# Gated linear attention outputs turned by VectorE in 32x32 blocks instead of by TensorE

## The chip, the cores and the metric

The kernel runs on one core of one Trainium2 chip. The metric is device time in microseconds (us), as the median of several runs; a separate profiled execution gives the trace that is read here.

## What is computed

One step of a hybrid decoder layer, for a prompt of 1024 tokens and 8 sample tokens, with model width 1024. From the normalised input come, by one combined input projection, the inputs of three branches: gated linear attention (GLA), multi-scale pooling and cross-attention. Each branch is gated, projected, gated again and summed; then one output projection, a residual and a final norm. What the change touches is the end of the first branch:

```python
o, S = gla_chunked(q, k, v, log_a, S0)                # 4 heads, key width 128, value width 256
o = rmsnorm(o, gla_gain.reshape(GLA_HEADS, GLA_DV))   # per head, times a gain for each channel
br_gla = o * jax.nn.silu(gla_g)
...
bproj = jnp.einsum('btnw,nwd->btnd', branches, w_branch)
```

## The kernel before

The heavy products run in float32r, each as three matmuls of a high and a low part (`mm3`, lines 241 to 243). The input projection is done in 40 column pairs (`Pair`), each as seven products (`run_product`, j = 0 to 6) of sums and differences of weight blocks (names a11, a12, s1 to s4, a22, with h and l for the parts). Results stand with channels on partitions and time along the free dimension, in tiles named c; GpSimd (POOL) stores them to scratch in DRAM. Only about two tiles c are in use at a time. Each c is written in four pieces (L611 and L628, then L637 and L647) out of PSUM tiles named px, of which there are six.

Between the products of the projection stand small steps of the other branches, as filler on TensorE. `fill` takes steps from two streams by a count of slots and of costs that the generators `yield`, so the order of TensorE and of the loads on SyncE (SP) is written out by the program. The order on VectorE, ScalarE and POOL is made by a scheduler. The GLA runs in 16 chunks, four heads by four chunks of 256 tokens, in the middle of the program. For a chunk, `gla_gates` makes the decays, `gla_within` the masked scores (tile ak holds their high and low part and the transposed key), `gla_recur` the recurrence with the state st and the outputs. The outputs leave `gla_recur` as tile `on` with tokens on partitions (two blocks of 128 tokens by 256 channels), scaled by the norm on ScalarE (L973, two instructions for a chunk). `gla_out` turns them: four 128x128 TensorE transposes against an identity into a small PSUM tile (L987; the small PSUM tiles, pz, are two), two ScalarE copies to tile `go` with the head's gain as scale (L989), and one store of 256 KB to the scratch `mixsc` (L990), channels by time.

Later, for the eight gate pairs of each branch (`Pair` with `gated`), `mixed` loads the stored half rows, 128 channels by 512 tokens (L662, tile mix), and `finish` multiplies them by the SiLU of the gate (L574). The products go to `brsc`. In the last stage `branch_k` loads them again and `split` makes the high part on ScalarE (L222) and the low part on VectorE (L223) for the branch projection. The branches are projected in the order cross-attention, GLA, pooling.

The value projection already has a block transpose: pairs with `turned` transpose a 128x512 tile on VectorE in 32x32 blocks (L581, tile vt), and four stores of a quarter of it (L584) put the blocks in place.

Of the kernel before, what the change touches and what calls it, by code (L numbers as in the profile page):

```python
# [14 lines left out]
AF = mybir.ActivationFunctionType  # L15
ALU = mybir.AluOpType
AX = mybir.AxisListType

P = 128
D = 1024  # L20
T = 1024
# [3 lines left out]
NH = 4  # L25
DK = 128
DV = 256
# [6 lines left out]
CT = 256  # L34
# [13 lines left out]
def trunk_kernel(ctx: ExitStack, tc: tile.TileContext,  # L48
# [3 lines left out]
    nc = tc.nc  # L52
# [46 lines left out]
    def PZ():  # L99
        return ps.tile([P, 512], F32, tag="pz", name="pz", bufs=2)  # L100
# [13 lines left out]
    def R(shape, dt=F32, name="r"):  # L114

        return shaped(wk.tile([P, 512], dt, tag="ring", name=name, bufs=NR), shape)
# [20 lines left out]
    ident = cp.tile([P, P], F32, name="ident")  # L137
# [27 lines left out]
    ngain, ggain, pscale, bav = vec[:, 0:8], vec[:, 8:16], vec[:, 16:24], vec[:, 24:28]  # L165
# [35 lines left out]
    def scratch(n, name, shape):  # L201
        return [dr.tile(list(shape), F32, name=f"{name}{i}") for i in range(n)]
# [6 lines left out]
    q_scr, k_scr = (scratch(2, s, PAIR) for s in ("qsc", "ksc"))  # L209
    vt_scr = scratch(NH, "vtsc", (T, DV))  # L210
    u_scr, xq_raw = (scratch(4, s, PAIR) for s in ("usc", "xqsc"))
    mix_scr = [scratch(4, f"mixsc{n}_", (P, 2, T)) for n in range(3)]
    m_scr = [scratch(4, f"msc{n}_", PAIR) for n in range(3)]
    br_scr = [scratch(4, f"brsc{n}_", PAIR) for n in range(3)]

# [3 lines left out]
    def split(dst_hi, dst_lo, src, scale=None):  # L219

        if scale is None:
            last["hi"] = nc.scalar.activation(dst_hi, src, AF.Copy)  # L222
            last["lo"] = nc.vector.tensor_tensor(dst_lo, src, dst_hi.bitcast(F32), op=ALU.subtract)  # L223
        else:
            nc.scalar.activation(dst_hi, src, AF.Copy, scale=scale)
            nc.vector.scalar_tensor_tensor(dst_lo, src, scale, dst_hi.bitcast(F32), op0=ALU.mult, op1=ALU.subtract)
# [319 lines left out]
    def run_product(n):  # L546

        i, j = seq[n]
        p = pairs[i]

        def saved(acc, c, name):
            r = Q(name)
            nc.scalar.activation(r, acc[c][:, :QT], AF.Copy)  # L553
            return r

        def piece(t, h, c):
            return t[:, h, c * QT:(c + 1) * QT]

        def diagonal(x, e):

            if e == 0:
                return x[:, 0:16].rearrange("p (a b) -> p a b", b=4)[:, 0:4:3]
            return x[:, 4:12].rearrange("p (a b) -> p a b", b=4)

        def finish(t, e):
            rows = (slice(0, 4, 3), slice(1, 3))[e]
            if p.s0 is not None:
                nc.gpsimd.tensor_copy(diagonal(smp[:, NS * p.s0:], e), t[:, :, 512:HT])
            if p.gated:
                n, g = p.gated  # L570
                for i in range(2):
                    ch, hf = divmod((0, 3, 1, 2)[2 * e + i], 2)
                    m = p.mix[e][i]
                    nc.vector.tensor_tensor(t[:, i, :512], t[:, i, :512], m, op=ALU.mult)  # L574
                ss = diagonal(brs[n].rearrange("p k b -> p (k b)")[:, 2 * NS * g:], e)
                nc.vector.tensor_tensor(t[:, :, 512:HT], t[:, :, 512:HT], ss, op=ALU.mult)
            if p.turned:
                for i in range(2):
                    ch, hf = divmod((0, 3, 1, 2)[2 * e + i], 2)
                    r = R([512], name="vt")  # L580
                    nc.vector.transpose(r, t[:, i, :512])  # L581
                    for q in range(4):
                        c0 = ch * P + 32 * q
                        nc.gpsimd.dma_start(out=p.dst[512 * hf:512 * hf + 512, c0:c0 + 32].rearrange("(t r) c -> r t c", r=32),  # L584
                                            in_=r[32 * q:32 * q + 32].rearrange("r (t c) -> r t c", c=32))
                return
            nc.gpsimd.dma_start(out=p.dst[:, rows, :], in_=t)

        def gate(t, h):
            if p.gated:  # L590
                act(t[:, h], t[:, h], AF.Silu)

        def mixed(e):

            if p.gated:
                n, g = p.gated
                for i in range(2):
                    ch, hf = divmod((0, 3, 1, 2)[2 * e + i], 2)
                    p.mix[e].append(loaded(mix_scr[n][g][:, ch, 512 * hf:512 * hf + 512], [512], "mix"))

        if j == 0:
            p.x = [PX() for _ in range(2)]
            p.r1, p.mix = [], ([], [])
            for c in product(p.x, n, True):
                p.r1.append(saved(p.x, c, "r1"))
                yield
        elif j == 1:
            y = [PX() for _ in range(2)]
            p.e1 = E([2, HT], name="c1")
            for c in product(y, n, True):  # L610
                nc.vector.tensor_tensor(piece(p.e1, 0, c), y[c][:, :QT], p.r1[c], op=ALU.add)  # L611
                if c:
                    gate(p.e1, 0)
                yield
        elif j == 2:
            p.r2 = []
            for c in product(p.x, n, False):
                p.r2.append(saved(p.x, c, "r2"))
                yield
        elif j == 3:  # L620
            p.z = [PX() for _ in range(2)]
            mixed(0)
            for c in product(p.z, n, True):
                yield
        elif j == 4:
            for c in product(p.x, n, False):
                r3 = saved(p.x, c, "r3")
                nc.vector.tensor_tensor(piece(p.e1, 1, c), p.z[c][:, :QT], r3, op=ALU.add)  # L628
                if c:
                    gate(p.e1, 1)  # L630
                    finish(p.e1, 0)
                yield
        elif j == 5:
            p.e2 = E([2, HT], name="c2")
            mixed(1)
            for c in product(p.z, n, False):
                nc.vector.tensor_tensor(piece(p.e2, 0, c), p.z[c][:, :QT], p.r2[c], op=ALU.add)  # L637
                if c:
                    gate(p.e2, 0)
                yield  # L640
        else:
            for c in product(p.x, n, False):
                dst = piece(p.e2, 1, c)
                if p.gated:
                    act(dst, p.x[c][:, :QT], AF.Silu)
                else:
                    nc.scalar.activation(dst, p.x[c][:, :QT], AF.Copy)  # L647
                if c:
                    finish(p.e2, 1)
                yield  # L650
# [6 lines left out]
    def mix_chunk(n, h, c):  # L657
        return mix_scr[n][h][:, :, c * CT:(c + 1) * CT]

    def loaded(src, shape, name, alloc=None):  # L660
        t = (alloc or R)(shape, name=name)
        nc.sync.dma_start(out=t, in_=src)  # L662
        return t
# [316 lines left out]

    def gla_out(h, c):
        on, _ = gla["o", h, c]
        g = R([2, CT], name="go")
        t = PZ()
        for i in range(2):
            for j in range(2):
                nc.tensor.transpose(t[:, i * CT + j * P:i * CT + (j + 1) * P], on[:, j, i * P:(i + 1) * P], ident)  # L987
        for i in range(2):
            nc.scalar.activation(g[:, i], t[:, i * CT:(i + 1) * CT], AF.Copy, scale=ggain[:, 2 * h + i:2 * h + i + 1])  # L989
        nc.gpsimd.dma_start(out=mix_chunk(0, h, c), in_=g)  # L990

    def gla_rows(h):

# [309 lines left out]
    with tc.issue_after(last["hi"].ins), tc.issue_after(last["lo"].ins):  # L1303
        prepare(1)
        for j in (4, 6):
            r = squares(x_t[j:j + 2], 4 + j)
# [35 lines left out]
    def branch_k(n, k):  # L1342
        hi, lo = E([2, HT], F32R, name=f"bh{n}"), E([2, HT], F32R, name=f"bl{n}")
        for hf in range(2):
            row = br_scr[n][k // 2][:, 2 * (k % 2) + hf]
            raw = loaded(row[:, :512], [512], "brr")
            split(hi[:, hf, :512], lo[:, hf, :512], raw)
        nc.sync.dma_start(out=brs[n][:, k].rearrange("p (h b) -> p h b", h=2),
                          in_=br_scr[n][k // 2][:, 2 * (k % 2):2 * (k % 2) + 2, 512:HT])
        split(hi[:, :, 512:HT], lo[:, :, 512:HT], brs[n][:, k].rearrange("p (h b) -> p h b", h=2))  # L1350
        return hi.rearrange("p h t -> p (h t)"), lo.rearrange("p h t -> p (h t)")
# [59 lines left out]
    for u, (o, n, d) in enumerate(units):  # L1411
# [4 lines left out]
        w, sig, acc = inputs.pop(u)  # L1416
# [56 lines left out]
    for hf, order in enumerate(ORDERS):  # L1473
        for tb in order:
            m = P if tb < 8 else NS
# [12 lines left out]
            if hf == 0:  # L1488
                x = (E([D], name="y") if tb < 8 else RAW("ys").rearrange("p a b -> p (a b)"))[:m]
                nc.sync.dma_start(out=x, in_=x_p[tb * P:(tb + 1) * P] if tb < 8 else x_s)  # L1490
                rows_[tb], sums[tb] = x, wk.tile([P, 4], F32, tag="yq", name="yq", bufs=9)[:m]
            x, sq = rows_[tb], sums[tb]
# [5 lines left out]
            n, a = hf, 0  # L1498
            for b in ends:
                t = ts if tb == 8 else begun.pop(0) if begun else PX()  # L1500
# [13 lines left out]
                n, a = n + 1, b  # L1514
# [3 lines left out]
            if end:  # L1518
                r = rstd_of(sq[:, 2:3], 1.0 / D, more=so_far)
# [41 lines left out]
```

## Time and profile before

| | |
|---|---|
| median of three runs | 1450.72 us (1450.0 to 1452.0) |
| the profiled execution | 1452.08 us, span 1450.2 us |
| granted TensorE clock | 0.999 |
| TensorE busy | 1421.7 us, 98% of the span |
| VectorE / ScalarE / POOL busy | 906.0 / 689.2 / 194.9 us |
| first and last transpose of `gla_out` on TensorE | 418.8 and 750.9 us |
| DMA | 259.42 MB, 179 GB/s on the mean |

A row of the groups and of the sources gives line, engine, operation, tiles as out<-in, and the count; then durations in ns (min/median/max), or the busy time in us, the mean of one in ns, and the idle time of the engine ahead of them with what ended it. A row of the timeline gives start and duration in us, and in brackets the idle time ahead and its releaser. PE is TensorE's matmul, PEld its weight load, DVE VectorE, ACT ScalarE.

### The profile page before, as it was taken

What the parts mean: (1) busy time and instruction counts of PE and PEld (TensorE: products, weight loads), DVE (VectorE), ACT (ScalarE), POOL (GpSimd) and SP (SyncE); (2) the same over time, 40 slices, a digit from 0 to 9 for tenths busy, and PEclk for the clock granted to TensorE, in tenths of its full rate; (3) what the DMA queues carried; (4) which work ended last, traced back from release to release, by engine and by line L of the source; (5) the groups of instructions that cost most, each with busy time, mean ns of one, the idle gap of its engine ahead of it and who ended that gap; (6) DMA issues with size and microseconds to landing.
All of it is one profiled execution on the core that took longest, in us unless ns stands there. A gap on an engine that the chain in (4) does not pass through costs nothing.

```text
span 1450.2 us, 28260 instructions
## 1 busy us (share of the span) xinstructions
PE 1421.7 (98%) x10753; PEld 1360.2 (94%) x10753; DVE 906.0 (62%) x2107; ACT 689.2 (48%) x1607; POOL 194.9 (13%) x353
## 2 busy tenths in 40 slices
PE   7999999998999999999999999999999999999998
PEld 6899999998899999999999999999999999999876
DVE  6956656666686767766756678785672434544436
ACT  6744435443465666656654445454472333233312
POOL 3112101124341111111111111110010000000000
PEclk9999999999999999999999999999999999999999
DMA  9346665666655453553544455455594677632633
GB/s 335 122 159 207 200 212 184 218 190 164 160 157 183 130 182 126 177 175 125 180 142 152 157 187 182 138 192 168 194 303 147 226 255 236 241 116 71 220 125 117
DMA packets 182739, 259.42 MB, mean 179 GB/s; under 512 B 21436, under 2 KB 131796, under 8 KB 182596
## 3 DMA queue, kind: packets, MB, share of 16 engines
q1 hardware_dynamic: 159900, 183.87, 41.4%
q0 software_dynamic: 22560, 73.56, 14.1%
q8 instruction: 84, 1.38, 0.4%
q14 instruction: 51, 0.42, 0.1%
q10 hardware_dynamic: 144, 0.20, 0.0%
HBM read 180.47 MB, written 77.56 MB: 178 GB/s over the span
## 4 chain that ended last, share of the span: by engine, by line
PE 86%; DMA 5%; DVE 5%; issue 2%; ACT 1%; SPq 0%; DVEq 0%; POOL 0%; ACTq 0%
PE px L241 25%; PE px L242 24%; PE px L243 24%; DMA qb<-xqs 2%; PE pz L243 2%; PE pz L242 2%; PE pz L241 2%; DMA raw<-in_w_in_dram 2%; DVE kc L769 1%; PE pz L403 1%; PE pz L955 1%; PE pz L936 1%; PE pz L809 1%; PE pz L938 1%; DVE ws L304 0%
## 5 line engine op out<-in xcount | busy, mean ns | idle before, releaser
L243 PE MATMUL px<-bh,wbl 128*128 128x384 f32 (+1 forms) x576 | 184.1, 320 | 0.0
L242 PE MATMUL px<-bl,wbh 128*128 128x384 f32 (+1 forms) x576 | 184.1, 320 | 0.0
L241 PE MATMUL px<-bh,wbh 128*128 128x384 f32 (+1 forms) x576 | 183.7, 319 | 0.0
L553 ACT ACTIVATE r<-px 128x258 f32<-128x258 f32 x240 | 90.0, 376 | 45.6 <-PE px L243 45.0
L241 PEld LDWEIGHTS px<-bh,wbh 128*128 128x128 f32 x576 | 108.3, 188 | 0.0
L242 PEld LDWEIGHTS px<-bl,wbh 128*128 128x128 f32 x576 | 108.2, 188 | 0.0
L243 PEld LDWEIGHTS px<-bh,wbl 128*128 128x128 f32 x576 | 108.2, 188 | 0.0
L241 PE MATMUL px<-ot,s1h 128*128 128x258 f32 x320 | 93.9, 293 | 0.0
L241 PE MATMUL px<-ot,s3h 128*128 128x258 f32 x320 | 93.4, 292 | 0.0
L241 PE MATMUL px<-o,s4h 128*128 128x258 f32 x320 | 93.2, 291 | 0.2 <-DVE c L628 0.2
L241 PE MATMUL px<-o,a11h 128*128 128x258 f32 x320 | 92.9, 290 | 0.0
L241 PE MATMUL px<-o,a12h 128*128 128x258 f32 x320 | 92.9, 290 | 0.0
L241 PE MATMUL px<-ot,a22h 128*128 128x258 f32 x320 | 92.9, 290 | 0.0
L241 PE MATMUL px<-ot,s2h 128*128 128x258 f32 x320 | 92.3, 288 | 0.0
L242 PE MATMUL px<-o,a11h 128*128 128x258 f32 x320 | 91.0, 284 | 0.3 <-DVE o L223 0.3
L243 PE MATMUL px<-o,a11l 128*128 128x258 f32 x320 | 90.6, 283 | 0.0
L242 PE MATMUL px<-ot,a22h 128*128 128x258 f32 x320 | 90.5, 283 | 0.0
L242 PE MATMUL px<-ot,s2h 128*128 128x258 f32 x320 | 90.0, 281 | 0.5 <-DVE ot L223 0.5
L243 PE MATMUL px<-ot,s3l 128*128 128x258 f32 x320 | 90.5, 283 | 0.0
L243 PE MATMUL px<-o,a12l 128*128 128x258 f32 x320 | 90.4, 283 | 0.0
L242 PE MATMUL px<-o,a12h 128*128 128x258 f32 x320 | 90.4, 283 | 0.0
L243 PE MATMUL px<-ot,s1l 128*128 128x258 f32 x320 | 90.4, 282 | 0.0
(470 smaller groups left out, 4616.0 us busy)
## 6 DMA issues: line engine op xcount, KB each, us to landing
raw<-in_w_in_dram SPq DMA_DIRECT2D x80, 512.0 KB, 4.0
msc<-c POOLq DMA_DIRECT2D x24, 516.0 KB, 4.3
brsc<-c POOLq DMA_DIRECT2D x24, 516.0 KB, 4.0
sig<-msc SPq DMA_DIRECT2D x24, 516.0 KB, 6.6
mix<-mixsc SPq DMA_DIRECT2D x48, 256.0 KB, 4.5
brr<-brsc SPq DMA_DIRECT2D x48, 256.0 KB, 5.2
wbr<-in_w_branch_dram SPq DMA_DIRECT2D x24, 512.0 KB, 6.1
acc<-sig POOLq DMA_DIRECT2D x16, 516.0 KB, 5.3
```

Of the source, the lines that this page charges most:

```text
L241: nc.tensor.matmul(out, lhsT=lh, rhs=rh, start=start, stop=False, skip_group_check=more)
L242: nc.tensor.matmul(out, lhsT=lh, rhs=rl, start=False, stop=False, skip_group_check=more)
L243: nc.tensor.matmul(out, lhsT=ll, rhs=rh, start=False, stop=stop, skip_group_check=more)
L403: nc.tensor.matmul(t[:, :DV], lhsT=memT[k // 2][:, k % 2, a * P:(a + 1) * P], rhs=raw[k // 2][:, k % 2], start=k == 0, stop=k == NK - 1)
L553: nc.scalar.activation(r, acc[c][:, :QT], AF.Copy)
L769: nc.vector.tensor_tensor_reduce(kc[:, a, :], kc[:, a, :], qb[:, bb, :], scale=1.0, scalar=0.0, op0=ALU.mult, op1=ALU.add, accum_out=sc[:, ...
L809: nc.tensor.matmul(t[32 * j:32 * j + 32, :DV], lhsT=pm[:, a, 4 * i + j, :], rhs=vc[j][:, a, :], start=a == 0, stop=a == 1)
L936: nc.tensor.matmul(t[0:64, 0:P], lhsT=ki[:, 0:64], rhs=qi, start=True, stop=True)
L938: nc.tensor.transpose(t[:, P:2 * P], kt, ident)
L955: nc.tensor.matmul(to, lhsT=kiqi[:, 1, cs], rhs=st, start=False, stop=True)
```

## The change

`gla_out` no longer uses TensorE, PSUM and ScalarE. One VectorE instruction transposes the chunk's 128x512 tile in 32x32 blocks, so that partition 32q+r holds channel 32b+r of the tokens 32q to 32q+31 of both token blocks j, for all eight channel blocks b. Four stores of 64 KB, one for each q, place these blocks in a new scratch `onsc`, in runs of 64 numbers (256 bytes). In that scratch a channel's 512 tokens lie together, but in the order q, chunk, token block. `mixed` reads the 512 numbers as before; `finish` multiplies through a view that puts the order right, in pieces of 32. The gain, which the removed ScalarE copies carried, becomes the scale of the first branch's `split` in `branch_k`: ScalarE's copy gets a scale, and VectorE's subtraction becomes a scalar-tensor-tensor instruction.

```diff
-    mix_scr = [scratch(4, f"mixsc{n}_", (P, 2, T)) for n in range(3)]
+    mix_scr = [None if n == 0 else scratch(4, f"mixsc{n}_", (P, 2, T)) for n in range(3)]
+    on_scr = scratch(NH, "onsc", (DV // 32, 32, 2, 4, 2, 64))
...
                     m = p.mix[e][i]
-                    nc.vector.tensor_tensor(t[:, i, :512], t[:, i, :512], m, op=ALU.mult)
+                    if n == 0:
+                        x = m.rearrange("p (q w k) -> p w q k", q=4, w=4)
+                        y = t[:, i, :512].rearrange("p (w q k) -> p w q k", q=4, w=4)
+                        nc.vector.tensor_tensor(y, y, x, op=ALU.mult)
+                    else:
+                        nc.vector.tensor_tensor(t[:, i, :512], t[:, i, :512], m, op=ALU.mult)
...
-                    p.mix[e].append(loaded(mix_scr[n][g][:, ch, 512 * hf:512 * hf + 512], [512], "mix"))
+                    src = (mix_scr[n][g][:, ch, 512 * hf:512 * hf + 512] if n else
+                           on_scr[g][4 * ch:4 * ch + 4, :, hf].rearrange("b r q c x -> (b r) (q c x)"))
+                    p.mix[e].append(loaded(src, [512], "mix"))
...
     def gla_out(h, c):
         on, _ = gla["o", h, c]
-        g = R([2, CT], name="go")
-        t = PZ()
-        for i in range(2):
-            for j in range(2):
-                nc.tensor.transpose(t[:, i * CT + j * P:i * CT + (j + 1) * P], on[:, j, i * P:(i + 1) * P], ident)
-        for i in range(2):
-            nc.scalar.activation(g[:, i], t[:, i * CT:(i + 1) * CT], AF.Copy, scale=ggain[:, 2 * h + i:2 * h + i + 1])
-        nc.gpsimd.dma_start(out=mix_chunk(0, h, c), in_=g)
+        g = R([512], name="go")
+        nc.vector.transpose(g.rearrange("p (b j k) -> p j b k", j=2, k=32), on.rearrange("p j (b k) -> p j b k", k=32))
+        for q in range(4):
+            nc.gpsimd.dma_start(out=on_scr[h][:, :, c // 2, q, c % 2].rearrange("b r x -> r b x"),
+                                in_=g[32 * q:32 * q + 32].rearrange("r (b x) -> r b x", b=8))
...
-            split(hi[:, hf, :512], lo[:, hf, :512], raw)
+            split(hi[:, hf, :512], lo[:, hf, :512], raw, None if n else ggain[:, k:k + 1])
```

How it moves instructions is seen at three places. The lines of the changed program are numbered a few higher.

TensorE at the last chunk, before: L1043 are the matmuls of the GLA's sample tokens, the others products of the projection.

```order
L243 MATMUL px<-o_501,a12l 128x258
L1043 MATMUL pz<-s_10022,pm 32x256 x2
L1043 MATMUL pz<-s_10026,pm 32x256 x2
L987 MATMUL pz<-ident,on 128x128 x4
L241 MATMUL px<-ot_705,s2h 128x258
L242 MATMUL px<-ot_706,s2h 128x258
```

The same place in the changed program:

```order
L244 MATMUL px<-o_501,a12l 128x258
L1048 MATMUL pz<-s_9980,pm 32x256 x2
L1048 MATMUL pz<-s_9984,pm 32x256 x2
L242 MATMUL px<-ot_705,s2h 128x258
L243 MATMUL px<-ot_706,s2h 128x258
```

The four transposes are gone and nothing else of TensorE's order has moved, here and at the other fifteen places.

VectorE at the second chunk, before: st is the GLA state, c a projection result, s the sample states, a11l and s4l low parts of weight factors, ws a sum of weight blocks.

```order
L304 TENSOR_TENSOR ws<-raw 128x512
L960 SCALAR_TENSOR_TENSOR st<-st,decp,pz 128x256
L611 TENSOR_TENSOR c_5848<-px,r_5720 128x258
L223 TENSOR_TENSOR a11l<-raw,a11h 128x512
L1026 SCALAR_TENSOR_TENSOR s_5963<-vb,smp,s_5963 128x256 x2
L223 TENSOR_TENSOR s4l<-ws,s4h 128x512
```

The same place in the changed program:

```order
L305 TENSOR_TENSOR ws<-raw 128x512
L968 SCALAR_TENSOR_TENSOR st<-st,decp,pz 128x256
L992 STREAM_TRANSPOSE go<-on 128x2x8x32
L224 TENSOR_TENSOR a11l<-raw,a11h 128x512
L619 TENSOR_TENSOR c_5845<-px,r_5703 128x258
L619 TENSOR_TENSOR c_5845<-px,r_5717 128x258
L1031 SCALAR_TENSOR_TENSOR s_5957<-vb,smp,s_5957 128x256 x2
L224 TENSOR_TENSOR s4l<-ws,s4h 128x512
```

The block transpose stands behind the state update, and the two additions into c stand behind it and a11l. At most of the other chunks, too, the transpose follows the state update or the next instruction.

POOL at the fifth chunk, before: s are sample states on their way out, usc and msc the scratch of projection results.

```order
L1027 DMA out_dram<-s_6882 128x2x256
L1027 DMA out_dram<-s_6886 128x2x256
L990 DMA mixsc_1_175<-go 256x1x256
L568 COPY smp<-c_6866 128x8
L587 DMA usc_169<-c_6866 128x1032
L587 DMA msc_0_194<-c_6975 128x2x516
```

The same place in the changed program:

```order
L1032 DMA out_dram<-s_6870 128x2x256
L994 DMA onsc_183<-go 32x8x64 x4
L569 COPY smp<-c_6854 128x8
L593 DMA usc_169<-c_6854 128x1032
L1032 DMA out_dram<-s_6874 128x2x256
L593 DMA msc_0_194<-c_6960 128x2x516
```

Four stores stand in place of one, ahead of the store of the result c, and one store of a sample state has moved behind that.

## The prediction

> **What bounds the kernel now.** I read four views in this order: the page's engine shares, the windows by stage, the waits of TensorE, and the timeline where the transposes stand.
>
> ```profile
> PE 1421.7 (98%) x10753; PEld 1360.2 (94%) x10753; DVE 906.0 (62%) x2107; ACT 689.2 (48%) x1607; POOL 194.9 (13%) x353
> ```
> TensorE is busy for all but 28.5 us of the 1450.2 us span. In the windows the columns after the length are busy us (and instructions) of PE, PEld, DVE, ACT and POOL, then clock, DMA share and GB/s.
>
> ```profile
> 310.00:418.00 108.00, 100.07 (x833) 94.54 (x833) 73.71 (x194) 50.97 (x128) 46.84 (x77) 1.00 0.63 166
> 420.00:760.00 340.00, 338.30 (x2771) 322.48 (x2770) 233.72 (x622) 213.08 (x596) 46.23 (x76) 1.00 0.48 157
> 760.00:1035.00 275.00, 275.00 (x2305) 274.77 (x2304) 195.54 (x425) 128.55 (x273) 30.67 (x53) 1.00 0.52 168
> 1060.00:1400.00 340.00, 339.82 (x2099) 328.30 (x2098) 152.52 (x291) 116.33 (x197) 16.44 (x29) 1.00 0.60 196
> ```
> The GLA chunks run in 420 to 760. There PE idles 1.7 us, VectorE is used to 69%, POOL to 14%, and the clock is full. The two stages behind it have no PE idle to speak of (0.0 and 0.2 us), so time saved on PE before them reaches the end. The whole idle time of PE in the GLA stage is two waits:
>
> ```profile
> PE pz L987 <- ACT on L973: 1.2, 1, 1.2
> PE pz L936 <- DVE ak L223: 0.4, 1, 0.4
> ```
> The first is a wait of the very transposes that the change removes.
>
> **The PE transposes, removed: 64 of them.** The line's own row gives durations, the timeline gives what they cost in the stream:
>
> ```profile
> L987 PE MATMUL pz<-ident,on x64: 270/272/328, 418.8 to 750.9; 128*128 128x128 f32 x64
> ...
> 441.88 0.28 PE L243 MATMUL px<-ot,s2l 128*128 128x258 f32 x1
> 442.00 0.60 PE L987 MATMUL pz<-ident,on 128*128 128x128 f32 x4
> 442.35 0.36 PE L241 MATMUL px<-ot,s2h 128*128 128x258 f32 x1
> 442.55 0.28 PE L242 MATMUL px<-ot,s2h 128*128 128x258 f32 x1
> ```
> A product matmul is recorded as 0.28 us but one starts every 0.12 us: records overlap, and starts are what counts. From 441.88 to the second product matmul behind the transposes is 0.67 us; without them it would be two steps, 0.24. So four transposes cost 0.43 us, not 4 x 0.272 = 1.09. Fifteen chunks: 15 x 0.43 = 6.5 us.
>
> The TensorE page of the Trainium skill ("TensorE: Matmul & The Clock Gate", Part 4: PE-mode transpose) gives about 275 ns for such a transpose in a kernel and says that access latency makes up most of it. The recorded 272 ns agrees, but the overlap in the starts denies that it is the price; that way of charging is a rival below.
>
> The sixteenth chunk waits. Here it is beside an ordinary place with the same sample matmuls (L1043) ahead:
>
> ```profile
> 443.73 0.28 PE L243 MATMUL px<-ot,s2l 128*128 128x258 f32 x1
> 443.94 0.64 PE L1043 MATMUL pz<-s,pm 128*32 128x256 f32 x8
> ...
> 444.73 0.28 PE L242 MATMUL px<-ot,s1h 128*128 128x258 f32 x1
> ...
> 748.12 0.28 PE L243 MATMUL px<-o,a12l 128*128 128x258 f32 x1
> 748.33 0.64 PE L1043 MATMUL pz<-s,pm 128*32 128x256 f32 x8
> 750.20 0.95 PE L987 MATMUL pz<-ident,on 128*128 128x128 f32 x4 [1.23 <-ACT on L973]
> ...
> 751.10 0.28 PE L242 MATMUL px<-ot,s2h 128*128 128x258 f32 x1
> ```
> From product matmul to second product matmul it is 1.00 us at the ordinary place and 2.98 at the last chunk: 1.98 us go, transposes and wait together. What comes behind on PE (left factor s2) was made long before. Sum of this part: 6.5 + 2.0 = 8.5 us.
>
> **VectorE: 16 block transposes, added.** The same operation on the same 128x512 stands in the trace for the value rows, and so do stores of a quarter of a turned tile:
>
> ```profile
> L584 POOL DMA_DIRECT2D vtsc<-vt x64: 649/649/752, 310.5 to 418.4; - x64
> L581 DVE STREAM_TRANSPOSE vt<-c x16: 699/703/711, 309.5 to 413.4; 128x512 f32<-128x512 f32 x16
> ...
> DMA to landing us min/median/max: 2.3/3.1/6.8
> ...
> L990 POOL DMA_DIRECT2D mixsc<-go x16: 661/674/712, 421.8 to 752.7; - x16
> ```
> 16 x 0.70 = 11.2 us, lifting VectorE from 233.7 to about 245 of 340 us. The write order differs (blocks of two row groups interleaved), so 0.70 is the lower bound; twice that is my upper one, since no row shows this pattern. I take 0.70, because the rows of this size on VectorE all stand near it. Is it covered? In the second chunk the new order puts it behind the state update (st):
>
> ```profile
> 435.90 0.91 ACT L973 ACTIVATE on<-on,rr 128x256 f32<-128x256 f32 x2 [0.81 <-DVE rr L264]
> ...
> 440.24 0.47 DVE L960 SCALAR_TENSOR_TENSOR st<-st,decp,pz 128x256 f32<-128x256 f32 x1
> ...
> 442.07 0.69 DVE L223 TENSOR_TENSOR a11l<-raw,a11h 128x512 fp32r<-128x512 f32 x1 [0.88 <-ACT a11h L222]
> ```
> Its input was ready at 436.81, so VectorE won't stall on it, and 0.88 us of idle follow. What is queued behind and matters to PE is the split of the scores (ak), needed by the recurrence. The tightest of the later chunks:
>
> ```profile
> 458.47 0.42 DVE L223 TENSOR_TENSOR ak<-pz,ak 128x256 fp32r<-128x256 f32 x1 [0.45 <-ACT ak L222]
> ...
> 462.44 0.28 PE L241 MATMUL pz<-vsh,ak 128*128 128x256 f32 x1
> ```
> 3.55 us lie between its end and its use, five transposes' worth. One place has none: PE's 0.4 us wait at L936 is for this ak's read of the PSUM tile. With PE 0.43 us per chunk earlier and VectorE not, up to 0.4 us of the saving may end there. I charge 0.2.
>
> **Gone from ScalarE:** 32 PSUM copies with the head scale. They only relieve it (SP's queue keeps its order; eight of its pairs of loads read the new scratch). PSUM has one small tile fewer per chunk, so the others come free sooner.
>
> **POOL: 64 stores for 16.** 48 more at 0.65 us make 31 us, 46 to 77 of 340. Behind the four stand the stores of the projection results (c), and a result's tile can only be rewritten when its store has landed. The slowest such store and the next write of that kind of tile:
>
> ```profile
> L587 POOL DMA_DIRECT2D usc<-c x1: 725/725/725, 505.5 to 505.5; - x1
> ...
> DMA to landing us min/median/max: 6.7/6.7/6.7
> ...
> 517.42 0.75 DVE L611 TENSOR_TENSOR c<-px,r 128x258 f32<-128x258 f32 x2
> ```
> Landed at 512.2, rewritten at 517.4: 5.2 us of slack against 4 x 0.65 - 0.67 = 1.9 us of delay. Cost nothing; if POOL were slower, c would be late next. The bytes are the same 4 MB, in 256-byte runs for 1 KB; the value rows' stores with half that run landed in 3.1 us, and the readers of these tiles start after 820 us:
>
> ```profile
> L662 SPq DMA_DIRECT2D mix<-mixsc x48: 319/382/1510, 820.2 to 1067.1; - x48
> ...
> L574 DVE TENSOR_TENSOR c<-c,mix 128x512 f32<-128x512 f32 x48 | 32.8, 686 | 7.0 <-ACT c L75 6.6 <-ACT r L553 0.4
> ...
> L1529 DVE SCALAR_TENSOR_TENSOR y<-y,rr,fg 128x512 f32<-128x512 f32 x14 | 9.9, 749 | 0.2
> ```
> **Gate product and split.** 16 of the 48 products (L574) now read both operands in pieces of 32. Between nothing and a doubling that is 0 to 16 x 0.69 = 11 us of VectorE in a stage where it idles 79; I take nothing. 16 splits of the first branch become a scalar-tensor-tensor, 749 for 686 ns: 1.0 us, in a stage with VectorE idle for 187 of 340 us; ScalarE's half takes a scale. Both off the path.
>
> **The sum:** 8.5 - 0.2 = 8.3 us. The profiled execution took 1452.08 us, 1.9 around its span; it would take 1443.8. It stands 1.4 above the median of the three runs, 1450.72; from that median the forecast is 1442.4. Bounds of the saving: 10 (PE's 0.4 us wait also goes, and the ends of the runs differ by a microsecond) down to 4 (first rival).
>
> **Rivals.**
> *The saving is part handed to new waits.* VectorE is 0.70 us later per chunk wherever no idle follows, as here, where the new order puts the transpose between the last two rows:
>
> ```profile
> 511.53 0.47 DVE L960 SCALAR_TENSOR_TENSOR st<-st,decp,pz 128x256 f32<-128x256 f32 x1
> 511.92 0.68 DVE L304 TENSOR_TENSOR ws<-raw 128x512 f32<-128x512 f32 x1
> 512.52 0.48 DVE L1026 SCALAR_TENSOR_TENSOR s<-vb,smp,s 128x256 f32<-128x256 f32 x1
> ```
> If half the chunks gave back their 0.43 us, 3.4 us: 1445.8. For it: VectorE's chain ends PE's wait at L936. Against: only one such wait in 340 us. If all gave it back, nothing measurable would be left beyond the last chunk's 2 us: 1448.9.
>
> *Transposes charged by duration:* 64 x 0.272 = 17.4 us, and the last chunk's wait of 1.98 - 0.43 = 1.5: 1431.8. The starts speak against it.
>
> *Slower: the POOL queue.* If the stores hold POOL, c lands late, VectorE can't empty the PSUM tiles, PE stops. From the emptying to the next use of those tiles there is further cover:
>
> ```profile
> 470.26 0.42 DVE L611 TENSOR_TENSOR c<-px,r 128x258 f32<-128x258 f32 x1
> ...
> 476.61 0.28 PE L241 MATMUL px<-o,a11h 128*128 128x258 f32 x1
> ```
> 5.9 us, with the 5.2 above 11.1. To end 0.2% (2.9 us) slower, 16 chunks must wait 11.2 us, 0.7 each: four stores of (0.67 + 11.1 + 0.7) / 4 = 3.1 us decide it, against 0.65 measured while VectorE was 68% busy (first window); at 3.3 us, PE loses 1.4 x 16 = 23 us: 1465. The SBUF page of the Trainium skill ("SBUF — State Buffer", SBUF: two separate sides) has a rule against this change: GpSimd cannot write descriptors while VectorE holds their shared port, and a store of 620 ns took 3100. By that the sum would come out near 1452; the rows L584 show no such store.
>
> **How the numbers follow.** A measurement of this kernel tells 0.2% (2.9 us) from no change, so faster means under 1447.8. Likeliest, 1441 to 1444: 0.66. Part given back, 1444 to 1447.8: 0.21. All given back: 0.06. By duration: 0.01. POOL slower: 0.04, and 0.02 for a small slowing that I can't name, of which half stays within. So faster 0.88, same 0.07, slower 0.05. The range 1440.7 to 1446.8 leaves out those last cases and the end of the second.
>
> **What would show it.** Line L987 gone and product matmuls in steps of 0.12 us there; PE busy in the GLA stage 7 us lower; the wait for on (L973) gone from PE's waits; 16 transposes near 0.70 us on VectorE, none waiting for on; 64 stores near 0.65 us. PE waiting for ak, s or a factor's low part, or VectorE waiting for a store of c, would prove the sum wrong, as would a PE idle of over 2 us in that stage.

## The result, and the profile after

The changed kernel takes 1444.15 us (median of 4 runs, 1442.07 to 1445.01), the kernel before 1451.36 us beside it (4 runs): a ratio of 0.9949, 95% interval 0.9932 to 0.9966. The prediction was 1442.4 us, 1440.7 to 1446.8.

The page's engine shares after, busy us and share of the span:

```profile
PE 1417.4 (98%) x10689; PEld 1356.1 (94%) x10689; DVE 916.2 (63%) x2123; ACT 679.0 (47%) x1575; POOL 222.1 (15%) x401
```

TensorE has lost 64 matmuls (10753 before), VectorE has 10.2 us more work, ScalarE 10.2 less, POOL 27.2 more. The windows of the same four stretches, with the prediction's columns:

```profile
310.00:418.00 108.00, 102.37 (x851) 97.47 (x850) 74.36 (x195) 51.28 (x129) 44.92 (x74) 0.98 0.63 168
420.00:760.00 340.00, 340.00 (x2785) 324.49 (x2784) 250.03 (x659) 206.23 (x575) 74.28 (x127) 1.00 0.53 164
760.00:1035.00 275.00, 275.00 (x2304) 274.77 (x2304) 195.83 (x420) 128.84 (x272) 30.65 (x53) 1.00 0.51 165
1060.00:1400.00 340.00, 339.82 (x2068) 326.79 (x2067) 149.18 (x285) 113.00 (x189) 15.64 (x28) 1.00 0.59 192
```

In the GLA stage TensorE is busy for 340.00 of 340 us (338.30 before): both of its waits are gone, the one of the removed transposes for `on` and the 0.4 us for `ak` at the scores. VectorE and POOL have taken the work over without TensorE waiting for either. Of the signs that the prediction named, PE's busy time in the stage fell by 7.6 us (from 337.3 to 329.7, between the matmuls of the table below); the page's total fell by only 4.3, since matmuls at a lower clock count as busy for longer (13 fill two microseconds where 19 did, in the windows of the last section). The first row's clock, 0.98 where it was 1.00, is taken up further down.

What the new instructions cost, from the rows of the sources (min/median/max ns; L992 is the block transpose, L994 its stores, L578 the gate product in pieces of 32, L580 the plain ones):

```profile
L992 DVE STREAM_TRANSPOSE go<-on x16: 702/705/715, 421.2 to 745.0; 128x512 f32<-128x512 f32 x16
L994 POOL DMA_DIRECT2D onsc<-go x64: 582/585/629, 423.9 to 747.7; - x64
L578 DVE TENSOR_TENSOR c<-c,mix x16: 683/686/694, 913.4 to 994.0; 128x512 f32<-128x512 f32 x16
L580 DVE TENSOR_TENSOR c<-c,mix x32: 684/691/697, 820.9 to 1072.4; 128x512 f32<-128x512 f32 x32
```

And TensorE's timeline where the last chunk stood. Before, the place between product a12 and product s2 took 2.98 us:

```profile
742.72 0.28 PE L244 MATMUL px<-o,a12l 128*128 128x258 f32 x1
742.93 0.64 PE L1048 MATMUL pz<-s,pm 128*32 128x256 f32 x8
743.50 0.39 PE L242 MATMUL px<-ot,s2h 128*128 128x258 f32 x1
743.72 0.28 PE L243 MATMUL px<-ot,s2h 128*128 128x258 f32 x1
```

From the product matmul at 742.72 to the second one behind, at 743.72, it is 1.00 us, the length of the ordinary place in the prediction.

Matmul starts mark the stages more sharply than fixed windows. I took the start of the same three matmuls in each trace: the product with s2 ahead of the GLA (414.8 us before), the product with s1 behind its last chunk (753.8), the first matmul of the branch projection (1078.0). The table, worked out from those starts and the spans, serves for the experiments too:

| kernel | ahead of the GLA | GLA | pooling | rest |
|---|---|---|---|---|
| before | 414.8 | 339.1 | 324.2 | 372.3 |
| changed | 416.7 | 329.7 | 324.2 | 372.6 |
| changed, run again | 416.3 | 329.7 | 324.2 | 372.3 |
| transposes of `on` put back | 413.6 | 339.7 | 323.9 | 372.2 |
| transposes of the identity added | 413.7 | 337.5 | 324.0 | 372.3 |
| ScalarE's copies put back | 416.2 | 331.6 | 325.6 | 372.3 |
| stores issued twice | 416.2 | 331.3 | 330.0 | 372.3 |
| twice, but not at the end | 411.6 | 330.6 | 324.2 | 373.2 |
| the keys turned too | 420.6 | 336.4 | 324.2 | 372.3 |
| cross-attention's end spread out | 411.1 | 330.3 | 332.9 | 372.2 |
| the same, plan raised to 499 | 409.8 | 331.6 | 324.2 | 372.2 |

The GLA stage became 9.3 us shorter and the two behind it kept their lengths. The profiled execution lost 1.9 us ahead of the stage, where the change has no instruction.

### The profile page after: what moved, and what is told of

Read it like the earlier page. It is cut to its first block, busy times and chain, and to the rows that moved or that the text cites. A ratio compares the mean times of both kernels' runs of the same rounds, so it can differ in the third digit from the quotient of the medians.

```text
span 1443.3 us, 28179 instructions
## 1 busy us (share of the span) xinstructions
PE 1417.4 (98%) x10689; PEld 1356.1 (94%) x10689; DVE 916.2 (63%) x2123; ACT 679.0 (47%) x1575; POOL 222.1 (15%) x401
## 4 chain that ended last, share of the span: by engine, by line
PE 88%; DMA 5%; DVE 5%; issue 1%; ACT 1%; SPq 0%; POOL 0%; DVEq 0%; ACTq 0%; POOLq 0%
PE px L242 25%; PE px L243 25%; PE px L244 25%; DMA qb<-xqs 3%; PE pz L244 2%; PE pz L243 2%; PE pz L242 2%; DMA raw<-in_w_in_dram 1%; DVE kc L777 1%; PE pz L963 1%; PE pz L404 1%; PE pz L944 1%; PE pz L817 1%; PE pz L946 1%; PE pz L907 0%
## 5 line engine op out<-in xcount | busy, mean ns | idle before, releaser
L242 PE MATMUL px<-ot,s1h 128*128 128x258 f32 x320 | 94.1, 294 | 0.0
L243 PE MATMUL px<-ot,s1h 128*128 128x258 f32 x320 | 90.8, 284 | 0.0
```

Of the source, the lines that this page charges most:

```text
L242: nc.tensor.matmul(out, lhsT=lh, rhs=rh, start=start, stop=False, skip_group_check=more)
L243: nc.tensor.matmul(out, lhsT=lh, rhs=rl, start=False, stop=False, skip_group_check=more)
```

## The experiments

Each ran against the kernel before on the same chip, on three chips in all; the median of the kernel before lies between 1451.1 and 1452.8 us there. So ratios compare better than times across experiments; "over the changed kernel" means over its rerun, 1441.75 us.

**The changed kernel, run again.** Nothing is edited; it is the base for the others.

> The changed kernel again, timed beside the experiments. Path theory (the gain is the TensorE steps of the 64 transposes and the last chunk's wait, everything added is hidden): 8.3 us below before, some 0.3 of them uncertain. Eaten-gain theory (VectorE or POOL give back a part): 7 us or less below.

Measured: 1441.75 us (1441.27 to 1444.18) against 1451.44, ratio 0.993 (0.9916 to 0.9944). The gain is 9.7 us here and 7.2 in the first comparison; the prediction's 8.3 lies between. The intervals overlap.

**TensorE's transposes put back beside the new way.**

```diff
         g = R([512], name="go")
+        t = PZ()
+        for i in range(2):
+            for j in range(2):
+                nc.tensor.transpose(t[:, i * CT + j * P:i * CT + (j + 1) * P], on[:, j, i * P:(i + 1) * P], ident)
```

Their result is not used.

> The changed kernel with the 64 TensorE transposes of the outputs put back, into a small PSUM tile that nothing reads; ScalarE's copies stay away, the block transposes and stores stay. Path theory: all of it comes back, 15 x 0.43 + 2.0 = 8.5 us above the changed kernel, at before's time. Relief theory (the gain came from ScalarE's 32 copies and from the small PSUM tiles that come free sooner): it stays within 1.5 us of the changed kernel.

Measured: 1449.85 us, ratio 0.9992 (0.998 to 1.0003), 8.1 over the changed kernel. All the rest of the change is in it, so nearly the whole gain is TensorE's. ScalarE's copies stay away here, and the GLA stage still takes 339.7 us, as long as before (339.1): in that stage the relief of ScalarE gained nothing that can be seen.

**The same transposes, of the identity instead of `on`**, so that they wait for no data:

```diff
+                nc.tensor.transpose(t[:, i * CT + j * P:i * CT + (j + 1) * P], ident, ident)
```

> As the run with the transposes put back, but they turn the identity, so that they wait for no output. Path theory: 16 x 0.43 = 6.9 us above the changed kernel, and 1.5 us below the run that turns the outputs, because the last chunk's wait does not come back. Charging by recorded duration: 64 x 0.272 = 17.4 us above. Relief theory: within 1.5 us of the changed kernel.

Measured: 1449.53 us, ratio 0.9984 (0.9975 to 0.9992), 7.8 over the changed kernel; its GLA stage is 7.8 longer too. The 1.5 us that were expected between this kernel and the last one are 2.1 us in their profiled GLA stages (337.5 and 339.7) but 0.3 in the medians, so the runs don't confirm them. TensorE's waits in 415 to 780 us, of the kernel with transposes of `on` and then of this one (line waited at, releaser, us in total, times, longest):

```profile
PE pz L944 <- DVE ak L224: 1.8, 2, 1.3
PE pz L996 <- ACT on L981: 0.4, 1, 0.4
```

```profile
PE pz L944 <- DVE ak L224: 0.4, 1, 0.4
```

Without the 0.4 us wait, 64 transposes cost 7.4 us, 0.46 for each four. The price read from starts was 0.43; the price by duration would have been 17.4 us in all. That rival has fallen.

**A second block transpose for each chunk**, its result unused:

```diff
+        nc.vector.transpose(R([512], name="g2").rearrange("p (b j k) -> p j b k", j=2, k=32),
+                            on.rearrange("p j (b k) -> p j b k", k=32))
```

> The changed kernel with a second block transpose of each chunk's outputs on VectorE, into a tile that nothing reads: 16 x 0.70 = 11.3 us more of VectorE in the GLA stage, some 265 of 335 us. Path theory: hidden, within 0.7 us of the changed kernel. Eaten-gain theory (VectorE's added work delays TensorE): at least 0.3 us per transpose shows, 5 us or more.

Measured: 1442.02 us, ratio 0.994 (0.9927 to 0.9953). Another 11 us on VectorE cost nothing measurable; the new work on VectorE is covered with as much again to spare.

**ScalarE's 32 scaled copies put back:**

```diff
+        g2 = R([2, CT], name="g2")
+        for i in range(2):
+            nc.scalar.activation(g2[:, i], on[:, i], AF.Copy, scale=ggain[:, 2 * h + i:2 * h + i + 1])
```

> The changed kernel with ScalarE's work put back: two scaled 128x256 copies for each chunk, from the outputs into a tile that nothing reads, 32 x 0.5 = 16 us of ScalarE; TensorE and PSUM untouched. Path theory: within 0.7 us of the changed kernel. Relief theory: most of the 7 us come back.

Measured: 1443.06 us, ratio 0.9941 (0.9927 to 0.9955), 1.3 over the changed kernel. The intervals overlap, so the runs don't settle it, but in its one trace the GLA and pooling stages are 3.3 us longer together, and it has waits that the changed kernel lacks:

```profile
PE pz L1066 <- ACT os L1060: 1.3, 1, 1.3
PE px L242 <- DVE c L636: 0.8, 2, 0.5
PE pz L944 <- DVE ak L224: 0.4, 1, 0.4
```

**The kernel before with only the gain moved** into the first branch's split:

```diff
-            nc.scalar.activation(g[:, i], t[:, i * CT:(i + 1) * CT], AF.Copy, scale=ggain[:, 2 * h + i:2 * h + i + 1])
+            nc.scalar.activation(g[:, i], t[:, i * CT:(i + 1) * CT], AF.Copy)
...
-            split(hi[:, hf, :512], lo[:, hf, :512], raw)
+            split(hi[:, hf, :512], lo[:, hf, :512], raw, None if n else ggain[:, k:k + 1])
```

> The kernel before with one part of the change: the head's gain moved from ScalarE's copies of the outputs into the first branch's split, everything else as before. Path theory: within 0.5 us of before. Rival: the 16 scalar-tensor-tensor splits show, 16 x 0.06 = 1 us above.

Measured: 1450.84 us, ratio 0.9996 (0.9987 to 1.0005): nothing, as the prediction had it.

**Each store four times**, the last three to scratch that nothing reads:

```diff
+            for scr in no_scr:
+                nc.gpsimd.dma_start(out=scr[h][:, :, c // 2, q, c % 2].rearrange("b r x -> r b x"),
+                                    in_=g[32 * q:32 * q + 32].rearrange("r (b x) -> r b x", b=8))
```

> The changed kernel with every store of a turned quarter issued four times, three of them to scratch that nobody reads: 16 stores or 9.4 us of POOL for each chunk, 192 x 0.585 = 112 us more, and 12 MB more of DMA. Path theory with the cover that the prediction worked out (5.2 us until a result tile is rewritten and 5.9 us until its PSUM tiles are needed): within 1 us of the changed kernel. POOL rival, if the cover is only the first 5.2 us: some 3.5 us of TensorE wait at most chunks, 20 us or more.

Measured: 1517.21 us, ratio 1.0461 (1.044 to 1.0481), 75 us over the changed kernel. Four stores at 0.58 are 2.3 us in place of one, under the 3.1 us that the prediction had called decisive, and the loss was far beyond its 23 us. TensorE waits for 53 us in 415 to 830 us, and the granted clock is 0.96 from 415 to 820 us, some 16 us more (0.04 x 405). The stores did not get slower, by their source row:

```profile
L995 POOL DMA_DIRECT2D onsc<-go x64: 582/582/637, 420.9 to 818.0; - x64
```

TensorE waits for the results c (its waits in 415 to 780 us):

```profile
PE px L243 <- DVE c L620: 32.0, 7, 8.4
PE px L243 <- ACT c L656: 12.9, 4, 4.3
```

One such wait in the timelines of POOL, VectorE and TensorE, in this order:

```profile
473.25 0.56 POOL L594 DMA_DIRECT2D usc<-c  x1
...
489.61 0.72 POOL L594 DMA_DIRECT2D usc<-c  x1
```

```profile
479.47 0.69 DVE L225 TENSOR_TENSOR s4l<-ws,s4h 128x512 fp32r<-128x512 f32 x1 [2.17 <-ACT s4h L224]
...
487.56 0.42 DVE L225 TENSOR_TENSOR ak<-pz,ak 128x256 fp32r<-128x256 f32 x1
487.90 0.75 DVE L620 TENSOR_TENSOR c<-px,r 128x258 f32<-128x258 f32 x2
```

```profile
488.37 0.39 PE L243 MATMUL px<-o,a11h 128*128 128x258 f32 x1 [2.67 <-DVE c L620]
```

TensorE waits for the addition into c. That addition waits for no store: no idle time stands ahead of it, and the last store of a c tile before it, issued at 473.25 us, landed at 477.5 us, 10 us earlier. VectorE even idled 2.17 us before 479.47. The addition just stands late in VectorE's order, behind the scores' split. In the traces 111 of VectorE's 2123 instructions stand elsewhere in its order than in the changed kernel. Nor does a store hold up the rest of the stage: of all the idle time of VectorE and ScalarE in 415 to 830 us, a landing store ended 0.8 us. So what TensorE waits for isn't a full POOL queue but results that stand late in the order that the scheduler made of the same work with twelve more stores per chunk in it. Only one of these waits was followed through, and that the scheduler counts the stores' time on POOL when it makes the order is argued, not shown.

**Each store twice.** The edit is the one above with one scratch. In the traces 30 of VectorE's instructions stand elsewhere than in the changed kernel. (The 113 and 733 of the expectation count lines of another listing, for this kernel and the one above.)

> The changed kernel, with each of the 64 stores of block-transposed outputs issued twice (the second into a scratch tensor that nothing reads), so that POOL issues 64 more stores of about 0.58 us, 37 us more in all. With four times the stores the time rose by 75 us, and the trace put that on VectorE's rows, which stood in another order; here VectorE's order differs from the changed kernel's in 113 rows only, against 733 there. Theory of the order: POOL itself has room, so the time stays within about 2 us of the changed kernel's 1442 to 1444. Rival, POOL's own load: the cost grows with the stores, a third of 75 us, so some 25 us more, about 1467.

Measured: 1451.45 us, ratio 0.9998 (0.9988 to 1.0008). Both theories missed: the whole gain is gone, but not 25 us. By the table 1.6 us are lost in the GLA stage and 5.8 behind it. TensorE's waits in 415 to 780 us show the second part:

```profile
PE pz L243 <- ACT dfh L224: 3.3, 1, 3.3
PE pz L945 <- DVE ak L225: 1.2, 2, 0.7
PE pz L244 <- DVE dfl L225: 0.3, 1, 0.3
```

dfh and dfl are the parts of the first pooling windows. Behind the first of these waits the clock is at half for 3.4 us (windows view, clock in the column behind POOL's), which costs (1 - 0.71) x 4 = 1.2 us in the window shown, so that 4.8 of the 5.8 us are accounted for:

```profile
768.00:772.00 4.00, 4.00 (x27) 4.00 (x27) 1.32 (x3) 2.01 (x5) 0.68 (x1) 0.71 0.74 212
```

Why the windows are late is seen on POOL's timeline, in the changed kernel and then in this one:

```profile
745.96 2.34 POOL L994 DMA_DIRECT2D onsc<-go  x4 [4.45 <-DVE rv L253]
751.73 0.54 POOL L1137 DMA_DIRECT2D out_dram<-hr  x1 [3.44 <-ACT hr L1136]
752.26 0.18 POOL L1147 MEMSET u<- 128x16 f32 x2
755.61 0.74 POOL L593 DMA_DIRECT2D msc<-c  x1 [3.17 <-DVE c L636]
```

```profile
751.33 0.58 POOL L998 DMA_DIRECT2D nosc<-go  x1
753.03 0.54 POOL L1141 DMA_DIRECT2D out_dram<-hr  x1 [1.11 <-ACT hr L1140]
756.89 0.74 POOL L594 DMA_DIRECT2D msc<-c  x1 [3.33 <-DVE c L637]
757.62 0.18 POOL L1151 MEMSET u<- 128x16 f32 x2
```

And on VectorE's timeline, again in the changed kernel and then in this one:

```profile
756.25 0.43 DVE L1165 TENSOR_TENSOR sw<-u 128x271 f32<-128x271 f32 x1
```

```profile
762.94 0.69 DVE L306 TENSOR_TENSOR ws<-raw 128x512 f32<-128x512 f32 x1
763.55 0.43 DVE L1169 TENSOR_TENSOR sw<-u 128x271 f32<-128x271 f32 x1
```

The zeroing of the windows' first columns (u) has changed places with the store of c, which waits 3.33 us for VectorE (not 3.9, as the next expectation has it). POOL stands idle for these 3.33 us, so what holds the zeroing back is its place in the order, not POOL's load. The zeroing comes 5.4 us later, and the first window sum (sw), which starts at 756.25 us in the changed kernel, stands at 763.55, behind six instructions, from the low part of s2 to the sum ws above, that follow it there.

**Each store twice, except in the last two chunks of the last head**, which restores the end of the stage:

```diff
-            for scr in no_scr:
+            for scr in (no_scr if (h, c) < (NH - 1, 2) else []):
```

> As the kernel that issues each of the 64 stores twice (1451.45 us), but the last two chunks of the last head store once again, so that 56 stores are added and not 64. In the kernel with all of them doubled the stage of the gated linear attention was only 1.6 us longer than in the changed kernel, and 5.8 us were lost right behind it: there POOL zeroes the pooling windows' first columns (L1147 of the changed kernel, L1151 there) 5.4 us later and behind the store of a projection result that waited 3.9 us for VectorE; the windows' sums, their split and TensorE's product then wait 3.3 and 0.3 us. Theory of the place: with the stage's end as in the changed kernel those 5.8 us come back, and 1443.5 to 1446 remain. Rival, the load of the stores as a whole: an eighth of them fewer gives back about an eighth of the 9 us lost, 1450.

Measured: 1443.29 us against 1452.75, ratio 0.9943 (0.9924 to 0.9962). With 56 of the 64 extra stores left, the gain is back. POOL's order at the place is the changed kernel's again (hr, zeroing, store of c):

```profile
747.36 0.54 POOL L1141 DMA_DIRECT2D out_dram<-hr  x1 [3.47 <-ACT hr L1140]
747.89 0.18 POOL L1151 MEMSET u<- 128x16 f32 x2
751.23 0.74 POOL L594 DMA_DIRECT2D msc<-c  x1 [3.16 <-DVE c L637]
```

And TensorE has one wait left in 415 to 780 us:

```profile
PE pz L945 <- DVE ak L225: 0.5, 1, 0.5
```

VectorE's order still differs, in 21 instructions, and the GLA stage is 0.9 us longer than the changed kernel's. So the place decided, not the number of the stores or a changed order as such: eight stores, 4.7 us of POOL, at the end of the stage cost what 56 elsewhere did not.

**The same idea for the keys.** The 32 TensorE transposes of the keys in `gla_within` were replaced in the same manner: a block transpose and four stores for a chunk, the keys loaded back and split before the recurrence.

```diff
+        nc.vector.transpose(kb, k)
+        for j in range(4):
+            nc.gpsimd.dma_start(out=kt_scr[4 * h + c][:, 32 * j:32 * j + 32].rearrange("(t r) c -> r t c", r=32),
+                                in_=kb[32 * j:32 * j + 32].rearrange("r (t c) -> r t c", c=32))
...
-        nc.tensor.transpose(t[:, P:2 * P], kt, ident)
```

> The changed kernel with the same treatment for the keys: the 32 TensorE transposes of the gated keys (two for each chunk) give way to 16 block transposes on VectorE (128x256), 64 stores of a quarter and 16 loads from scratch, split into parts from SBUF. Path theory: each transpose costs between a quarter of 0.43 us (as one of four) and the 0.26 to 0.28 us that the chain of before gives it, so 3.5 to 9 us below the changed kernel. Rival: the trip over DRAM (store 2.5 us, load 4 to 5 us to landing, and the loads queued behind it on SP) comes too late, and TensorE waits as long as it saves or longer: no gain or slower.

Measured: 1457.16 us, ratio 1.0045 (1.0029 to 1.0061), 15 us slower than the changed kernel for less work on TensorE. By the table some 4 us are lost ahead of the GLA and 6.7 in it. The largest of TensorE's waits in 370 to 790 us, which begins at 394 us, and one of the many smaller ones:

```profile
PE pz L1011 <- DVE ak L225: 3.6, 1, 3.6
...
PE pz L950 <- ACT pz L983: 1.6, 1, 1.6
```

These keys are needed within the stage, while the outputs are read from 903 us on, 155 us behind their last store. VectorE's order differs too: 221 of the changed kernel's 2123 instructions stand elsewhere. How much of the loss is the trip through DRAM and how much the order was not taken apart.

**Two tries at a version that beats both.** Ahead of the GLA, at the end of cross-attention, TensorE of the changed kernel waits 2.4, 1.5 and 1.1 us:

```profile
PE pz L803 <- DVE ps L798: 2.4, 1, 2.4
PE pz L243 <- DVE pTl L224: 1.5, 1, 1.5
PE pz L724 <- ACT xo L736: 1.1, 1, 1.1
```

The first try spreads the last two rounds:

```diff
                 if s + 2 < 16:
                     cross_fetch(*divmod(s + 2, 4))
+            else:
+                yield 3
```

> The changed kernel, with the last two rounds of cross-attention spread out: where no scores are left to be computed, as much of the products' work is put between the steps as stands there in the other rounds (a step of 3 in the order of the mixed-in work). In the changed kernel PE idles there 1.5, 1.1 and 2.4 us at 355 to 367 us, and the granted clock falls to half for 3.4 us right behind it. Theory: with products between them these waits go, up to 5.0 us, and the dip behind them, up to 1.7 us: about 1437 to 1440. Rival: the work that follows is pushed back and the waits come up later, at the end of the gated linear attention: no change, 1442 to 1444, or slower.

Measured: 1447.96 us, ratio 0.9977 (0.9963 to 0.9991). By the table the stretch ahead of the GLA is 5.7 us shorter, but the kernel with stores doubled except at the end, which lacks this edit, stands at 411.6 us as well (neither has the clock's dips of the last section); so little of it is shown to be the edit's. Where pooling begins 8.7 us are lost, on a load that came too late (waits) and on the clock behind it (windows):

```profile
PE pz L1129 <- DMA hist<-in_state_pool_dram: 2.6, 1, 2.6
```

```profile
754.00:758.00 4.00, 3.78 (x18) 3.81 (x18) 0.47 (x3) 0.31 (x1) 0.71 (x3) 0.50 0.43 162
```

The second also raises the plan's total (`WORK_A` from 493 to 499), so that nothing is left over at the end.

> The kernel whose last two rounds of cross-attention are spread out (1447.96 us), with the total work of the mixed-in stages in the order's plan raised from 493 to 499, so that the added steps are spread over all of it and nothing is left over at its end. In that kernel the part ahead of the gated linear attention was 5.7 us shorter than in the changed kernel, and 8.7 us were lost where pooling begins (a wait of 2.6 us for a load issued too late, and the clock at half behind it). Theory: the loss at the start of pooling goes and the gain stays, 1437 to 1440. Rival: the faster pace puts new waits elsewhere, 1442 to 1448.

Measured: 1442.95 us (1439.53 to 1445.63) against 1452.75, ratio 0.993 (0.991 to 0.995). The loss at pooling is gone and its profiled execution, 1439.53 us, is below every run of the changed kernel, but its interval holds both ratios of the changed kernel. A better version isn't shown.

## Why the prediction was right, and where its reasons were not

- *Four transposes cost 0.43 us, by starts.* Right in kind, a little low: 0.46 measured.
- *The last chunk's 1.98 us.* Right: the place shrank to the ordinary 1.00 us. With 15 x 0.46 = 6.9 us for the other chunks and the 0.4 us of the next point, that makes the stage's 9.3 us.
- *0.2 us charged for TensorE's wait for `ak`.* Wrong in sign: the 0.4 us wait vanished. It came back with the transposes (0.4), but also without them (0.6 in all with the second block transpose, 0.5 with stores doubled except at the end). It hangs on small shifts of the order; what decides it stays open.
- *VectorE's 11.2 us covered, gate product and split at nothing.* Right: 705 ns for a transpose, hidden even twice over; 686 ns for the product in pieces against 691; the moved gain alone a ratio of 0.9996.
- *ScalarE's copies only relieve it.* Open, perhaps 1 us: putting them back brought waits of 2.5 us in a profile and 1.3 us in the medians, within the intervals; with the transposes back and the copies away the stage was as long as before.
- *64 stores cost nothing.* Right for 64 at 585 ns, but in part by luck: the cover named for it was the wrong one. The prediction held 11.1 us of slack on c against the stores and put the turning point at 3.1 us per store. Two stores of 0.585 in place of one, 1.2 us, already gave everything back, most of it through the last two chunks. What the step missed is that POOL also zeroes the pooling windows right behind the last chunk, and that more POOL work changes the order the scheduler writes for VectorE and POOL, so a slack measured in the old order does not carry over. The changed kernel stands nearer to that edge than the prediction saw.
- *GpSimd kept from writing descriptors by VectorE.* The longest store took 629 ns with VectorE busy for 250 of 340 us. Of the 3100 ns that the Trainium skill ("SBUF — State Buffer", SBUF: two separate sides) tells of, these runs show nothing.
- *The sum, 8.3 us.* 7.2 and 9.7 were measured, with intervals of 4.9 to 9.9 and 8.1 to 12.2 us. Both hold the prediction's 8.3 and the stage's 9.3, so the runs can't tell these two apart; the clock (last section) adds to the spread.

## What to carry to other kernels

Price a TensorE instruction in a dense stream by how far it pushes the next start, not by its recorded length: here 0.43 us for four transposes recorded at 1.09. Moving such work to an engine with room pays where the result goes to memory and is read much later; where it is needed in the same stage, as the keys were, the same move lost (through the trip to memory, the order or both). When a scheduler orders the engines, look for every kind of work that stands behind the added one on its queue, the first step of the next stage above all, because slack read from the old order may not exist in the new one.

## What the runs showed of the hardware

The 1.9 us lost ahead of the first changed instruction come from TensorE's clock. Windows of 2 us, the clock in the column behind POOL's, before and then after:

```profile
124.00:126.00 2.00, 2.00 (x19) 2.00 (x18) 0.69 (x1) 0.60 (x3) 0.00 (x0) 1.00 0.85 228
126.00:128.00 2.00, 1.77 (x15) 1.56 (x13) 1.87 (x6) 1.44 (x4) 0.00 (x0) 1.00 0.94 362
```

```profile
124.00:126.00 2.00, 2.00 (x13) 2.00 (x13) 0.69 (x1) 0.26 (x1) 0.00 (x0) 0.63 0.78 167
126.00:128.00 2.00, 2.00 (x12) 2.00 (x11) 0.41 (x2) 1.27 (x5) 0.00 (x0) 0.52 0.99 372
...
366.00:368.00 2.00, 1.61 (x9) 1.62 (x10) 1.96 (x5) 1.21 (x4) 0.00 (x0) 0.71 0.95 323
368.00:370.00 2.00, 2.00 (x15) 1.42 (x17) 0.40 (x1) 0.00 (x0) 0.00 (x0) 0.50 0.03 9
```

Twice the granted clock fell to half for 3.4 us (a dip, from here on), each time behind short waits of TensorE, of which none was over 2.4 us. Each costs up to 1.7 us, (1 - 0.5) x 3.4. That the stretch ahead of the GLA differs by more than 3.4 us in the table has a second part: TensorE's idle time in 100 to 415 us, which goes from 11.6 us before to 9.1 with doubled stores except at the end. The rerun of the changed kernel had both dips, the identity kernel the second alone; the kernel before, the one with only the gain moved and the one with doubled stores except at the end had none. Up to 405 us the order on TensorE, VectorE, ScalarE and POOL is the same in all of these, so the execution decides, not the change.

What decides is where a wait falls on a fixed grid. In each of the 14 traces all dips, the one at the program's end among them, start a whole multiple of 3.413 us apart (in the trace after 124.50 and 366.85 us, 71 steps). Cut into the stretches of this grid, from 20 us on, TensorE idled at least 1.67 us in the stretch right ahead of each dip, but for two that only prolong one; and no stretch in which it idled over 1.91 us was without a dip behind it. So the changed kernel's 2.4 us wait at 364 us, whole in one stretch, cost a dip, and the 2.7 us wait at 360 us of the kernel before, which the grid cut into 1.61 and 1.13, cost none. This was read from the traces; no run set the grid's place. The Trainium skill ("TensorE: Matmul & The Clock Gate", Part 1: The HAM clock gate) tells of a free-running window of 3413 ns and of the half clock after an idle window. The length agrees; but here idling for about half of a window was enough.
